# A longer hold-back of gate tiles after attention, and a fourth raw weight buffer, in a two-layer pool and latent-attention trunk

## Chip, core and metric

The kernel runs on one core of one Trainium2 chip. The time is the device time of one execution in microseconds (us). Shown are the median and the extremes of several executions, and one execution more that was taken with the hardware profiler. TensorE is called PE in the profile, VectorE DVE, ScalarE ACT, GpSimd POOL, and SP is the engine whose queue issues nearly all DMAs here.

## What is computed

Two layers act on a residual stream of 528 tokens (16 learned tokens in front of 512) and 1024 channels:

```
h = rmsnorm(h_res, norm_gain[l])
proj = h @ w_in[l]
u_pool, z_pool, c_q, c_kv, k_rope, z_mla, g_pool, g_mla = jnp.split(proj, IN_SPLIT_POINTS, axis=-1)
y_pool = (pool_mix(u_pool, pool_w_group[l], pool_scale[l]) * jax.nn.silu(z_pool)) @ pool_w_up[l]
o_mla = mla(c_q, c_kv, k_rope, pos, q_a_norm_gain[l], kv_a_norm_gain[l], w_q_b[l], w_kv_b[l],
            q_norm_gain[l], k_norm_gain[l])
y_mla = (o_mla * jax.nn.silu(z_mla)) @ mla_w_up[l]
merged = jax.nn.sigmoid(g_pool) * y_pool + jax.nn.sigmoid(g_mla) * y_mla
h_res = h_res + merged @ w_out[l]
```

`mla` is causal attention with eight heads of width 96, normalised queries and keys, and a rotary part. The first 16 tokens are dropped from the output, so the second layer computes most projections for 512 columns only; the first does it for 528, in two halves of 264.

## The kernel before

Every projection is a row of tiles of 128 output channels, each named: `zm0` to `zm3` (the gate of the attention output), `gp0` to `gp7` (pool gate), `gm0` to `gm7` (attention gate), `mu0` to `mu7` (up projection of the attention output) and `o0` to `o7` (output projection) are the ones that matter here, and they come in that order in one list, `plan`. A product in float32 is made of three fp32r matmuls (`mm3`, lines 210 to 214): the high part of the weights with the high and the low part of the input, then the low part of the weights with the high part of the input.

Weights come in chunks of 128 x 512, that is four blocks of the contraction. Line 136 issues the DMA of a chunk from SP into a buffer of the tag `raw`. Lines 206 and 207 split it: ACT rounds it to `whi`, DVE subtracts to get `wlo`; the second-layer `mu` tiles with odd number put both into a buffer called `th` instead, which the attention also uses. A raw buffer is free again when DVE has finished its subtraction. There are three raw buffers and three each of `whi` and `wlo`. A tile of `zm`, `gp`, `gm` or `o` has two chunks, `mu` has one.

The results accumulate in PSUM buffers of the tag `mm`, of which there are four. For a `gm` tile DVE evacuates the bank (line 1058, a multiplication by the row norm) and ACT applies a tanh (line 1059); the bank is free after line 1058.

The list of tiles is a generator (`stream`) that gives up control after every six matmuls of 512 columns and reports a planned cost of 6 x 512 / 2.4 = 1280 ns. The attention code calls for such steps to fill in work: `fill_now(ns)` takes steps until their planned cost reaches `ns`; `gap()` adds `FILL` of the layer to a running due time and takes steps until the clock of planned costs has reached it, but it stops for good once the tile named in `RESERVE` is done. Each head has four gaps: two between its first and its last scores, two after its `prep` of the next head. So the tiles behind the `RESERVE` tile are kept for the end. There the code reads (lines 1216 to 1224):

```
self.pv(late)
if not self.last:
    self.meta_queries()
fill_now(TAIL[self.l])
late = self.parts(now)
fill_now(2600)
self.pv(late)
up("gm7")
flush()
```

The first `pv` is that of head 6, the second that of head 7. Between a head's softmax and its `pv` lies a round trip through DRAM that transposes the probabilities: a write (`pdr`, line 916), four reads (`attE`, line 924), the row sums out and back (`rdr`, lines 927 and 934) and the split of the result (`parts`, lines 972 and 973). All of it goes through SP's queue, in order, together with the raw weight chunks. After the second `pv`, line 1003 adds its two halves, and 6000 ns of planned cost later `part2` (lines 1008 to 1014) takes a PSUM bank, adds the part of the 16 learned tokens (line 1009), multiplies by the gate and splits the result, which is the last input of the `mu` tiles.

What is written down in this way is a priority. A scheduler walks through the program with a model of the engines' times and lets each engine take the first instruction in program order that is ready; so a matmul of a later tile can move ahead of an attention matmul whose input is late, and a DMA ahead of one that waits. The resulting order of each engine is fixed at compile time, and on the chip each engine's queue runs strictly in it.

Of the kernel before, what the change touches and what calls it, by code (L numbers as in the profile page):

```python
# [9 lines left out]
F32 = mybir.dt.float32  # L10
# [8 lines left out]
P = 128  # L19
# [31 lines left out]
G_H, G_CKV, G_CQ, G_QN, G_QR, G_KN, G_KR, G_PS = 0, 8, 10, 16, 17, 18, 19, 20  # L51
N_GAIN = 24

FILL = (2583.0, 2493.0)
RESERVE = ("gm3", "gm3")
LAG = 2000.0
TAIL = (9000.0, 9000.0)
SPL = 240
BACK = 7800.0
LATE = 13000.0  # L60
# [21 lines left out]
def trunk(ctx, tc, xT, xrow, mrow, pos, win, wkr, wqb, wkb, wvb, wgr, wpu, wmu, wout, gains, const, yT):  # L82
# [5 lines left out]
    wp = ctx.enter_context(tc.tile_pool(name="wp", bufs=2))  # L88
# [7 lines left out]
    def nm(s):  # L96
        uid[0] += 1
        return f"{s}_{uid[0]}"
# [38 lines left out]
        return raw  # L137

    def rawt():
        return wp.tile([P, 512], F32, tag="raw", name=nm("raw"), bufs=3)  # L140

    early.append(slot("rinv"))
    act.dma_start(early[0][:, 0:512], win[0, MT_CKV, :, 0:512])
    first = sp.dma_start(gn, gains)
    sp.dma_start(xb[:, 0, :T], xT[:, 0, :])
    early.append(fetch(win[0, MT_CKV + 1, :, 0:512], 512, rawt(), sp))
    sp.dma_start(xb[:, 1, :T], xT[:, 1, :])
    xt = [xb[:, k] for k in range(8)]
# [16 lines left out]
    def other_loads(made):  # L165
        for k in range(2, 8):
            behind(sp.dma_start(xb[:, k, :T], xT[:, k, :]), made)
            if k in (3, 4):
                raw = rawt()
                behind(sp.dma_start(raw, win[0, MT_CKV + k - 3, :, 512:1024]), made)  # L170
                early.append(raw)
        behind(sp.dma_start(cst, const), made)
        behind(sp.dma_start(posb[:, :T], pos.partition_broadcast(P)), made)
        dve.tensor_copy(maskw[:, 512 - P:], cst[:, C_MASK:C_MASK + P])
# [18 lines left out]
    def wload(src, n, spare, home=None):  # L193
        if home is not None:
            raw = home
            behind(sp.dma_start(raw, src), marks[-4])
        else:
            raw = early.pop(0) if early else fetch(src, n, rawt(), sp)
        loads[0] += 1
        marks.append(newest[0])  # L200
        if loads[0] <= 2 or spare:
            t = wide()
            hi, lo = t[:, 0:512], t[:, 512:1024]
        else:
            hi, lo = (wp.tile([P, 512], F32R, tag=t, name=nm(t), bufs=3) for t in ("whi", "wlo"))
        act.activation(hi[:, :n], raw[:, :n], AF.Copy)  # L206
        dve.tensor_sub(lo[:, :n], raw[:, :n], hi[:, :n].bitcast(F32))  # L207
        return hi, lo
# [87 lines left out]
    def fill(ns, limit):  # L296
        if due[0] is None:
            due[0] = clk[0]
        due[0] += ns
        while clk[0] < due[0] and limit not in done and step():  # L300
            pass

    def fill_now(ns):
        end = clk[0] + ns
        while clk[0] < end and step():
            pass
# [47 lines left out]
    class Layer:  # L354
# [804 lines left out]
        def gap(self):  # L1159
            fill(FILL[self.l], (self.l, RESERVE[self.l]))  # L1160

        def go(self, nxt):
# [54 lines left out]
# [4 lines that stand above are left out]
# [87 lines left out]
```

## Time and profile before

| | |
|---|---|
| median of 3 runs (lowest to highest) | 753.75 us (753.75 to 754.27) |
| the profiled execution | 755.48 us |
| its span, first to last instruction | 753.7 us |
| PE, PE weight loads, DVE, ACT, POOL busy | 748.1, 681.9, 562.3, 395.2, 241.8 us |
| granted PE clock over the span | 1.000 |

A row of a timeline gives the start from the beginning of the span, the duration, engine, line, operation, and the tiles as written `out<-in`; in brackets stands how long the engine had been idle and what ended it. Matmuls are pipelined, and their recorded ends are modelled, so their durations overlap: what a matmul costs is the distance from its start to the next start. A row of the chain of waits names what the end of the program hung on at that time. In the second layer the scores of the eight heads run from 555.87 us to 654.4 us, the last `gm` matmuls end at 682.0 us, and the first `mu` matmul is at 682.24 us.

### The profile page before, as it was taken

How to read it: one execution, taken by the hardware profiler on the slowest of the kernel's cores; microseconds unless marked ns; L12 is line 12 of the kernel's file. 1: busy time of each engine (PE TensorE's matmuls, PEld its weight loads, DVE VectorE, ACT ScalarE, POOL GpSimd, SP SyncE). 2: the span in 40 equal slices, each digit the busy share in tenths (PEclk: the TensorE clock that was granted, in tenths of full speed). 3: DMA queues.
4: the chain of work that ended last, by engine and by line, in shares of the span. 5: the costliest groups of instructions: out<-in, count | busy, mean ns of one | idle time of the engine just before them, and what ended most of it. 6: DMA issues, size and time to landing. Idle time of an engine off the chain costs nothing.

```text
span 753.7 us, 14317 instructions
## 1 busy us (share of the span) xinstructions
PE 748.1 (99%) x5010; PEld 681.9 (90%) x5010; DVE 562.3 (75%) x1214; ACT 395.2 (52%) x864; POOL 241.8 (32%) x294
## 2 busy tenths in 40 slices
PE   9999999999999999999999999999999999999998
PEld 9999899999999999999997898887788888887887
DVE  5588777658999987694367478678589999966942
ACT  6755656554656555543254456455445665554321
POOL 2126404704552520161130264038043526102400
PEclk9999999999999999999999999999999999999999
DMA  8633223434766576425643332233356666763462
GB/s 280 179 103 118 70 81 91 112 96 142 206 163 177 170 202 176 129 91 165 183 135 91 108 113 73 82 91 107 105 151 216 181 175 189 203 167 98 129 223 87
DMA packets 72798, 106.55 MB, mean 141 GB/s; under 512 B 14051, under 2 KB 34915, under 8 KB 72726
## 3 DMA queue, kind: packets, MB, share of 16 engines
q1 hardware_dynamic: 72582, 105.38, 47.8%
q8 instruction: 39, 0.64, 0.4%
q14 instruction: 33, 0.27, 0.1%
q10 hardware_dynamic: 144, 0.26, 0.1%
HBM read 89.76 MB, written 15.85 MB: 140 GB/s over the span
## 4 chain that ended last, share of the span: by engine, by line
PE 94%; DMA 4%; SPq 1%; DVE 1%; ACT 0%; issue 0%; ACTq 0%; DVEq 0%
PE mm L211 28%; PE mm L213 28%; PE mm L212 28%; PE S L211 2%; PE S L213 2%; PE S L212 2%; DMA raw<-wmu 1%; PE o L994 1%; DMA rdr<-rs 1%; PE o L997 1%; PE S L891 1%; PE S L538 1%; PE S L504 0%; DMA raw<-win 0%; DMA cq<-rdr 0%; DMA xb<-xT 0%
## 5 line engine op out<-in xcount | busy, mean ns | idle before, releaser
L213 PE MATMUL mm<-hh,wlo 128*128 128x264 f32 (+2 forms) x1072 | 337.0, 316 | 0.0
L212 PE MATMUL mm<-hl,whi 128*128 128x264 f32 (+2 forms) x1072 | 336.4, 315 | 0.0
L211 PE MATMUL mm<-hh,whi 128*128 128x264 f32 (+2 forms) x1072 | 336.3, 315 | 0.0
L207 DVE TENSOR_TENSOR wlo<-raw,whi 128x512 fp32r<-128x512 f32 (+2 forms) x239 | 179.6, 754 | 87.5 <-ACT whi L206 83.9
L206 ACT ACTIVATE whi<-raw 128x512 fp32r<-128x512 f32 (+2 forms) x239 | 143.0, 600 | 167.3 <-PE mm L212 133.2
L211 PEld LDWEIGHTS mm<-hh,whi 128*128 128x128 f32 x1072 | 201.4, 188 | 14.1 <-DVE vt L704 0.8
L212 PEld LDWEIGHTS mm<-hl,whi 128*128 128x128 f32 x1072 | 201.6, 188 | 13.0
L213 PEld LDWEIGHTS mm<-hh,wlo 128*128 128x128 f32 x1072 | 200.9, 188 | 12.3
L652 POOL TENSOR_TENSOR racc<-racc,tmp 128x264 f32<-128x264 f32 (+1 forms) x15 | 14.9, 993 | 117.7 <-ACT tmp L651 117.7
L1069 POOL TENSOR_TENSOR tmp<-tmp,xb 128x264 f32<-128x264 f32 (+1 forms) x24 | 27.7, 1166 | 41.8 <-DVE tmp L1067 39.7
L821 POOL CAST qhl<-q 32x528 fp32r<-32x528 f32 (+1 forms) x32 | 27.6, 876 | 40.5 <-PE S L891 39.1
L843 DVE CUSTOM_DVE_ANT_0 S<-S,maskw,nqs 128x240 f32<-128x240 f32 (+4 forms) x80 | 37.9, 493 | 1.5 <-PE S L213 1.3
L211 PE MATMUL mm<-cq,whi 128*128 128x264 f32 (+1 forms) x108 | 34.7, 321 | 0.0
L212 PE MATMUL mm<-th,whi 128*128 128x264 f32 (+1 forms) x108 | 34.6, 321 | 0.0
L213 PE MATMUL mm<-u,wlo 128*128 128x264 f32 (+1 forms) x108 | 34.5, 320 | 0.0
L212 PE MATMUL mm<-cq,whi 128*128 128x264 f32 (+1 forms) x108 | 34.5, 321 | 0.0
L213 PE MATMUL mm<-cq,wlo 128*128 128x264 f32 (+1 forms) x108 | 34.5, 321 | 0.0
L211 PE MATMUL mm<-u,whi 128*128 128x264 f32 (+1 forms) x108 | 34.5, 319 | 0.0
L938 POOL TENSOR_TENSOR u<-u,cq 128x512 f32<-128x512 f32 x8 | 12.9, 1616 | 64.6 <-DMA cq<-rdr 41.2
L853 POOL COPY pm<-cq 128x16 f32<-128x16 f32 x32 | 17.9, 559 | 44.4 <-ACT cq L850 42.3
L850 ACT ACTIVATE cq<-S,bia 128x400 f32<-128x400 f32 (+2 forms) x48 | 24.4, 512 | 13.9 <-DVE bia L904 12.8
L973 DVE TENSOR_TENSOR attE<-attE,th 128x640 fp32r<-128x640 f32 x32 | 25.6, 828 | 6.1 <-ACT th L972 6.1
(305 smaller groups left out, 1401.2 us busy)
## 6 DMA issues: line engine op xcount, KB each, us to landing
raw<-win SPq DMA_DIRECT2D x143, 256.0 KB, 3.5
pdr<-attD SPq DMA_DIRECT2D x16, 640.0 KB, 3.6
attE<-pdr SPq DMA_DIRECT2D x64, 160.0 KB, 3.6
raw<-wout SPq DMA_DIRECT2D x32, 256.0 KB, 3.0
raw<-wpu SPq DMA_DIRECT2D x16, 256.0 KB, 2.7
raw<-wmu SPq DMA_DIRECT2D x16, 256.0 KB, 2.7
raw<-wqb SPq DMA_DIRECT2D x12, 256.0 KB, 2.6
xb<-xT SPq DMA_DIRECT2D x8, 264.0 KB, 5.6
```

The lines of the kernel that those rows point to most:

```text
L206: act.activation(hi[:, :n], raw[:, :n], AF.Copy)
L207: dve.tensor_sub(lo[:, :n], raw[:, :n], hi[:, :n].bitcast(F32))
L211: first = pe.matmul(out, wh, xh, start=start, stop=False)
L212: pe.matmul(out, wh, xl, start=False, stop=False)
L213: newest[0] = pe.matmul(out, wl, xh, start=False, stop=stop)
L652: self.acc_last = gp.tensor_add(self.acc[:, a:b], self.acc[:, a:b], t[:, :b - a])
L821: gp.tensor_copy(d[r0:r0 + 32, x0:T], f[gq:gq + 32, x0:T])
L843: return dve.tensor_tensor_reduce(out=sv, in0=sv, in1=mask, scale=nqs[:, i, h:h + 1], scalar=3e38, op0=ALU.add, op1=ALU.min, accum_out=bia ...
L850: act.activation(pv, sv, AF.Exp, scale=-1.0, bias=bia[:, i:i + 1], accum_out=rs[:, c:c + 1])
L853: gp.tensor_copy(pm[:, i, 16 * odd:16 * odd + 16], pt[i][:, 0:NM])
L973: dve.tensor_sub(got[:, a:b], f[:, a:b], hi[:, a:b].bitcast(F32))
L1069: gp.tensor_add(t[:, :b - a], t[:, :b - a], self.am[m][:, a:b])
```

## The change

The fill per gap of the second layer goes from 2493 to 2145 ns, its last tile before the hold-back from `gm3` to `gm2`, the fill ahead of the split of head 7 from 9000 to 14000 ns, and `raw` gets a fourth buffer, in both layers:

```
-FILL = (2583.0, 2493.0)
-RESERVE = ("gm3", "gm3")
+FILL = (2583.0, 2145.0)
+RESERVE = ("gm3", "gm2")
 LAG = 2000.0
-TAIL = (9000.0, 9000.0)
+TAIL = (9000.0, 14000.0)
...
     def rawt():
-        return wp.tile([P, 512], F32, tag="raw", name=nm("raw"), bufs=3)
+        return wp.tile([P, 512], F32, tag="raw", name=nm("raw"), bufs=4)
```

No instruction is added or removed; only their order and what they wait for can differ.

## Prediction

> **What bounds the kernel now.** The page first: the span, the engines' busy time, the shares of the chain that ended last.
>
> ```profile
> span 753.7 us, 14317 instructions
> PE 748.1 (99%) x5010; PEld 681.9 (90%) x5010; DVE 562.3 (75%) x1214; ACT 395.2 (52%) x864; POOL 241.8 (32%) x294
> PE 94%; DMA 4%; SPq 1%; DVE 1%; ACT 0%; issue 0%; ACTq 0%; DVEq 0%
> ```
>
> PE is the bound nearly everywhere. The change neither adds nor removes a matmul, so all that it can win is time in which PE stood still. The view of PE's waits, whole program, has three rows:
>
> ```profile
> PE mm L211 <- DVE cq L1058: 1.1, 1, 1.1
> PE wps L158 <- DVE na L774: 1.1, 1, 1.1
> PE S L994 <- ACT th L972: 0.2, 1, 0.2
> ```
>
> The second is the start of the program, before any input is there. The other two can be won. PE's timeline around the first of them:
>
> ```profile
> 686.16 0.40 PE L213 MATMUL mm<-q,th 128*128 128x512 f32 x1
> 687.70 0.47 PE L211 MATMUL mm<-q,whi 128*128 128x512 f32 x1 [1.14 <-DVE cq L1058]
> 688.01 0.39 PE L212 MATMUL mm<-kn,whi 128*128 128x512 f32 x1
> ```
>
> The normal distance between matmuls of 512 columns comes from the first and last of a run of 30 `gm` matmuls with nothing between them:
>
> ```profile
> 668.96 0.39 PE L211 MATMUL mm<-hh,whi 128*128 128x512 f32 x1
> ...
> 675.66 0.40 PE L213 MATMUL mm<-hh,wlo 128*128 128x512 f32 x1
> ```
>
> (675.66 - 668.96) / 29 = 0.231 us. The stall is therefore 1.54 - 0.23 = 1.31 us, and the matmul after it is another 0.31 - 0.23 = 0.08 us late: 1.39 us in all. It falls in the third `mu` tile. What led to it, in the chain of waits:
>
> ```profile
> 674.15 5.58 DMA raw<-wmu
> 679.75 0.64 ACT th L206
> 680.41 0.79 DVE th L207
> 681.22 2.70 DMA raw<-wmu
> 684.02 0.64 ACT th L206
> 684.69 0.68 DVE th L207
> 685.41 0.69 DVE tmp L1003
> 686.14 0.70 DVE wlo L207
> 686.86 0.70 DVE cq L1058
> 687.70 0.47 PE mm L211
> ```
>
> Read it from the bottom. PE needed the PSUM bank of the last `gm` tile, which had been computed by about 682.3 us but was evacuated only at 686.86 us (there are four `mm` banks: this one, that of `part2` at line 1009, and those of the first two `mu` tiles). DVE came so late because its queue is in order and stood at the subtraction of a `mu` chunk, whose DMA was issued only at 681.22 us, 0.02 us after another subtraction (680.41 + 0.79) had freed a raw buffer. So the stall is a raw buffer too few, passed on through SP, ACT and DVE to PE. The two DVE steps of head 7 and the second split in between lengthened it.
>
> The third row of PE's waits is a small case of the same in the first layer, where the head-7 split stands behind a weight chunk in ACT's queue:
>
> ```profile
> 303.38 0.28 PE L212 MATMUL mm<-hl,whi 128*128 128x264 f32 x1
> 303.50 0.28 PE L213 MATMUL mm<-hh,wlo 128*128 128x264 f32 x1
> 303.98 0.51 PE L994 MATMUL S<-th,vt 128*128 128x512 f32 x1 [0.19 <-ACT th L972]
> 302.04 0.64 ACT L206 ACTIVATE whi<-raw 128x512 fp32r<-128x512 f32 x1 [2.65 <-DMA raw<-win]
> 298.45 0.53 SPq L136 DMA_DIRECT2D raw<-win  x1
> ```
>
> The matmul before it is followed after 0.48 us, where one of 264 columns takes 0.12 us (303.38 to 303.50): about 0.35 us are lost.
>
> **The change part by part.** *Fourth raw buffer.* Each chunk DMA may be issued one free buffer earlier. For the chunk of 681.22 us the wait on the subtraction goes, and SP could have issued it right behind the chunk of 674.15 us and the three small reads that follow that. It then lands before the 684.02 us that ACT waited for, by up to the whole 2.70 us of its DMA; DVE reaches the bank that much earlier, more than 1.31 us. I take 0 to 1.39 us as the bounds of the gain and choose 1.39, because the next parts act on the same place. In the first layer the chunk of 298.45 us could go ahead of the row-sum read that SP had waited for: 0 to 0.35 us, and I take 0.35, since one buffer more is exactly one chunk ahead.
>
> *FILL, RESERVE, TAIL.* Counted in steps of 1280 ns, from the first gap of layer two, after `zm0`: 12 steps remain in `zm`, 32 in `gp`, 32 in `gm`. Before, 30 gaps lie ahead of the last scores: 30 x 2493 = 74790 ns, 59 steps; at the end of the loop 60, because `gm3` ends there and the limit holds (62.3 would be due). After: 30 x 2145 = 64350 ns, 51 steps, and 32 x 2145 = 68640 ns, 54 steps, short of the 56 at which `gm2` ends, so that limit never acts. Held back are 76 - 54 = 22 steps, five and a half tiles, against 16. The tail takes 11 steps for 14000 ns (8 for 9000), 3 for 2600, then the `pv` of head 7. So 22 - 14 = 8 steps come after it instead of 16 - 11 = 5: 3 x 6 x 0.231 = 4.2 us more between that `pv` and the first `mu`. The additions of line 1003 and `part2`, which in the chain above stand in the `mu` stage, then fall among `gm` tiles, and the bank of `part2` is no longer taken just ahead of `mu`. This too takes the 1.39 us away, by another road; the two do not add.
>
> What is moved is 8 steps, that is four weight chunks, from before the last scores to behind them. Each chunk takes along one DMA on SP, one ACT split and one DVE subtraction, every second one an evacuation. On SP these four pass behind the `pdr`, `attE` and `rdr` transfers of heads 6 and 7. The matmuls cost the same in either place, if PE has work in both. Whether it has is a question of DVE:
>
> ```profile
> core 0: us, PE busy (x) PEld busy (x) DVE busy (x) ACT busy (x) POOL busy (x), PEclk, DMA share, GB/s
> 556.00:654.40 98.40, 98.40 (x492) 83.10 (x490) 94.05 (x227) 60.81 (x145) 40.39 (x62) 1.00 0.63 182
> 654.40:682.00 27.60, 27.60 (x130) 22.50 (x129) 17.95 (x37) 13.38 (x30) 2.96 (x5) 1.00 0.64 164
> ```
>
> ```profile
> L207 DVE TENSOR_TENSOR wlo<-raw,whi 128x512 fp32r<-128x512 f32 x28 | 19.7, 703 | 2.3 <-ACT whi L206 2.3
> L1058 DVE TENSOR_TENSOR cq<-mm,rinv 128x512 f32<-128x512 f32 x3 | 2.0, 673 | 0.0
> ```
>
> From the first to the last scores 98.4 us of PE carry 94.05 us of DVE. The change takes 8 x 6 x 0.231 = 11.1 us of PE out, but only 4 x 0.703 + 2 x 0.673 = 4.2 us of DVE. Written as it stands, 87.3 us of PE would have to carry 89.9 us of DVE: 2.6 us short. My forecast counts this at nothing because the scheduler gives PE the next ready matmul, and later `gm` tiles move up into such holes, which undoes part of the hold-back; the cover is the 22 steps kept back, and DVE has 27.60 - 17.95 = 9.65 us free in the stretch after. Without that cover it costs 2.6 us, and 2.6 + (98.40 - 94.05) = 6.9 us if DVE keeps its idle time.
>
> Contention is in this too. The same DVE operation took 0.69 us alone and 1.11 us beside a cast on POOL:
>
> ```profile
> 609.73 0.69 DVE L667 SCALAR_TENSOR_TENSOR xb<-tmp,xb 128x512 f32<-128x512 f32 x1
> 625.77 1.11 DVE L667 SCALAR_TENSOR_TENSOR xb<-tmp,xb 128x512 f32<-128x512 f32 x1
> 625.68 0.66 POOL L821 CAST qhl<-q 32x512 fp32r<-32x512 f32 x1 [0.95 <-PE S L891]
> ```
>
> The Trainium skill (SBUF — State Buffer, section SBUF: two separate sides) says that DVE operations with two SBUF inputs and GpSimd operations that read SBUF shut each other out of a shared port for a whole instruction; these rows agree, with 0.42 us. By that rule a denser attention meets the same POOL work more often, by 98.4 / 87.3 = 1.13; on eight such operations at most 8 x 0.42 x 0.13 = 0.4 us more for DVE, so the shortage would be 3.0 and not 2.6 us. No bound below uses it.
>
> *The start.* The fourth buffer is empty at once, so a fourth chunk may slip into the queue while SP waits for the gains:
>
> ```profile
> GB/s 280 179 103 118 70 81 91 112 96 142 206 163 177 170 202 176 129 91 165 183 135 91 108 113 73 82 91 107 105 151 216 181 175 189 203 167 98 129 223 87
> 2.12 0.43 SPq L147 DMA_DIRECT2D xb<-xT  x1
> 3.42 0.80 SPq L167 DMA_DIRECT2D xb<-xT  x2
> 9.03 0.77 DVE L379 SCALAR_TENSOR_TENSOR hl<-xb,gn,hh 128x528 fp32r<-128x528 f32 x1 [0.90 <-ACT hh L377]
> 10.58 0.28 PE L212 MATMUL S<-hl,th 128*128 128x264 f32 x1
> ```
>
> SP is free between 2.55 and 3.42 us. A chunk of 256 KB at the 280 GB/s of the first slice is 0.94 us, by which the six later parts of the input would land later. The block made at 9.03 to 9.80 us is used at 10.58 us, so 0.78 us of it are covered there, less where an engine is already idle for it. Bounds 0 and 0.94 us; I take 0.2, nearer to the cover.
>
> **The sum**, against the profiled execution: 755.48 - 1.39 - 0.35 + 0.2 = 753.9 us. The median of the runs is 1.73 us below the profiled execution, so 752.2 us.
>
> **Rivals.** *A, forecast:* both stalls go. With all of the start's 0.94 us it is 753.75 - 1.74 + 0.94 = 753.0; without it 752.0; own range 751.9 to 753.1.
>
> *B, nothing comes of it:* another in-order queue takes the stall's place. For it: SP still sits in line behind the round trip of head 7, the chunk issued at 674.15 us took 5.58 us to land, and four more chunks are behind that trip now. Against it: 4.2 us of added cover. Time 753.75, give or take 1.
>
> *C, slower:* DVE becomes the bound from the first scores of layer two to the last. For it the 94.05 of 98.40 us; against it that PE found a ready matmul at every moment of this stretch. It decides where matmuls do not move up, that is where their own weight subtractions wait in the same full DVE queue. Price 2.6 to 6.9 us less the 1.74: 754.6 to 758.9, its middle 756.8 us.
>
> *D, slower for the first layer's order:* the fourth buffer shifts the chunk DMAs of the first layer's attention too, and a new hole appears in an order that has none now. One bank or chunk late is a stall like the present one, 1.39 us, two are 2.8: 753.75 to 755.2 with the gain of A taken off, 755.1 to 756.5 without it.
>
> **How the numbers follow.** A 0.50, B 0.15, C 0.25, D 0.10. A measurement of this kernel can tell about 0.2%, 1.51 us, from no change; faster means below 752.24. A's sum lies just there, so I give it 0.31 of faster and 0.19 of same; B is same at 0.14 and slower at 0.01; C is slower at 0.23, same at 0.02; D is half same, half slower at 0.10. That makes faster 0.31, same 0.40, slower 0.29. The range takes in all of A and B and C up to its middle: 751.8 to 756.8 us.
>
> **What would show it.** Right: no wait of PE on line 1058 near the first `mu` tiles; line 1009 of head 7 some steps before the last `gm` tile; about 22 steps, 30 us, of `gm` after the last gap, last scores some 6 to 11 us earlier; no wait before the head-7 `pv` of layer one. Wrong, towards C: waits of PE on lines 843, 850, 207 or 973 between the scores, with DVE at 99% there. Wrong, towards D or the start: new waits before 320 us or in the first 15 us. The forecast as a whole is wrong if PE's waits after the start add to more than 1 us.

## The result, and the profile after

| | before | after |
|---|---|---|
| median (lowest to highest), 22 runs each | 754.36 us (753.75 to 756.53) | 755.42 us (754.47 to 756.80) |
| ratio of after to before, 95% interval | | 1.0013 (1.0007 to 1.0019) |
| the profiled execution, its span | 755.48, 753.7 us | 756.46, 754.6 us |

The change makes the kernel slower by 0.13%, 1.0 us, inside the bound of 0.2% but clear of no change. The 22 runs of before include the three of the first table: two of those are the fastest of all, the third lies in the middle.

The page of the changed kernel, and the view of its PE waits over the whole program:

```profile
span 754.6 us, 14325 instructions
PE 749.3 (99%) x5010; PEld 682.3 (90%) x5010; DVE 559.2 (74%) x1214; ACT 395.4 (52%) x864; POOL 239.1 (32%) x294
```

```profile
PE wps L158 <- DVE na L774: 1.1, 1, 1.1
PE mm L213 <- DVE wlo L207: 0.5, 1, 0.5
PE mm L1009 <- DMA racc<-mdr: 0.4, 1, 0.4
PE mm L211 <- DVE u L587: 0.2, 1, 0.2
```

Both waits that I had counted on are gone, the one on line 1058 and the one of the first layer's head-7 `pv`. In their place stand a wait of the first `mu` tile for the low part of its weights, one of line 1009 for the read of the learned tokens' part, and a small one on line 587 in the first layer. The chain of waits of the changed kernel up to that `mu` tile (start, duration, what it hung on):

```profile
659.33 5.27 DMA pdr<-attD
...
665.99 3.73 DMA attE<-pdr
669.82 0.75 ACT th L972
670.59 0.69 DVE attE L973
671.33 0.82 DVE attE L973
672.15 0.61 DVE wlo L207
672.78 5.25 DMA raw<-wmu
678.06 0.65 ACT th L206
678.73 0.70 DVE th L207
679.45 2.62 DMA raw<-wmu
682.15 0.65 ACT th L206
682.82 0.70 DVE th L207
683.54 0.69 DVE cq L1058
684.24 0.61 DVE wlo L207
684.89 0.50 PE mm L213
```

It begins at head 7's round trip through DRAM: its write, its reads, and the split on ACT and DVE. Only then, in the same two queues, comes the split of a weight chunk, which frees a raw buffer; two chunk DMAs follow, each begun when a split had freed a buffer, and the low part of the first `mu` tile's weights is made behind them. So the next question was whether this end of the attention, or chance, or the buffer made the loss.

### The profile page after: what moved, and what is told of

It reads as the page before. It is cut to its first block, busy times and chain, and to the rows that moved or that the text cites. A ratio compares the mean times of both kernels' runs of the same rounds, so it can differ in the third digit from the quotient of the medians.

```text
span 754.6 us, 14325 instructions
## 1 busy us (share of the span) xinstructions
PE 749.3 (99%) x5010; PEld 682.3 (90%) x5010; DVE 559.2 (74%) x1214; ACT 395.4 (52%) x864; POOL 239.1 (32%) x294
## 4 chain that ended last, share of the span: by engine, by line
PE 95%; DMA 3%; DVE 1%; issue 0%; ACT 0%; SPq 0%; DVEq 0%; ACTq 0%
PE mm L213 28%; PE mm L211 28%; PE mm L212 28%; PE S L211 2%; PE S L213 2%; PE S L212 2%; DMA raw<-wmu 1%; PE o L994 1%; PE o L997 1%; DMA pdr<-attD 1%; PE S L891 1%; PE S L538 1%; PE wps L158 1%; DMA attE<-pdr 0%; PE S L504 0%
## 5 line engine op out<-in xcount | busy, mean ns | idle before, releaser
L207 DVE TENSOR_TENSOR wlo<-raw,whi 128x512 fp32r<-128x512 f32 (+2 forms) x239 | 175.8, 738 | 87.0 <-ACT whi L206 82.4
L821 POOL CAST qhl<-q 32x528 fp32r<-32x528 f32 (+1 forms) x32 | 25.1, 799 | 42.2 <-PE S L891 40.9
L973 DVE TENSOR_TENSOR attE<-attE,th 128x640 fp32r<-128x640 f32 x32 | 27.6, 882 | 4.3 <-ACT th L972 4.3
```

Source lines behind the costliest of these rows:

```text
L821: gp.tensor_copy(d[r0:r0 + 32, x0:T], f[gq:gq + 32, x0:T])
L973: dve.tensor_sub(got[:, a:b], f[:, a:b], hi[:, a:b].bitcast(F32))
```

## Experiments

The eleven were timed in three series (e1 to e4, e5 to e8, e9 to e11), each on one chip together with the kernel before, with 11 runs of each experiment; the median of before was 753.77, 753.77 and 753.64 us there. The ratio has its 95% interval. The column raw is the number of raw buffers. "Lost" is worked out from PE's starts in each trace: the distance from one matmul to the next less the 0.23 us that 512 columns take, ahead of the head-7 `pv` and in the first three `mu` tiles.

| kernel | FILL | TAIL | raw | gm matmuls between last scores and head-7 pv | lost: pv, mu | ratio |
|---|---|---|---|---|---|---|
| before, first profile | 2493 | 9000 | 3 | 81 | 0, 1.31 us | |
| e5 before again | 2493 | 9000 | 3 | 81 | 0, 0 | 1.0002 (0.9993 to 1.0010) |
| e1 | 2493 | 9000 | 4 | 81 | 0, 0 | 1.0003 (0.9994 to 1.0012) |
| e4 | 2493 | 14000 | 3 | 98 | 0, 0 | 0.9998 (0.9989 to 1.0007) |
| e8 | 2493 | 14000 | 4 | 98 | 0, 0 | 0.9996 (0.9987 to 1.0005) |
| e3 | 2145 | 9000 | 3 | 69 | 0.50, 0 | 1.0007 (0.9998 to 1.0016) |
| e2 | 2145 | 14000 | 3 | 69 | 0.61, 0 | 1.0007 (0.9998 to 1.0016) |
| e7 | 2145 | 9000 | 4 | 69 | 0.43, 0.85 us | 1.0015 (1.0006 to 1.0023) |
| after, first profile | 2145 | 14000 | 4 | 69 | 0.13, 0.67 us | 1.0013 (1.0007 to 1.0019) |
| e6 after again | 2145 | 14000 | 4 | 69 | 0.30, 0.46 us | 1.0008 (0.9999 to 1.0016) |
| e9 | 2145 | 18000 | 4 | 99 | 0, 0 | 1.0002 (0.9994 to 1.0011) |
| e11 | 2300 | 14000 | 4 | 91 | 0, 0 | 1.0001 (0.9992 to 1.0010) |
| e10 | 2493 | 4000 | 3 | 72 | 0.85, 0 | 1.0022 (1.0012 to 1.0032) |

The limit `gm2` has no run of its own: with `gm3` in its place in the changed kernel, the compiled program is the same, since 54 steps are due at the end of the loop and the limit lies at 56.

### The parts one by one: e1 to e4

e1, the buffer alone:

```
-        return wp.tile([P, 512], F32, tag="raw", name=nm("raw"), bufs=3)
+        return wp.tile([P, 512], F32, tag="raw", name=nm("raw"), bufs=4)
```

> The kernel before with the fourth raw buffer alone. Theory O (the loss lies in the new order that FILL and TAIL make, the buffer by itself helps): the first layer's wait ahead of the head-7 pv goes, and part of the wait on line 1058, so 0.4 to 1.7 us faster than before. Theory B (the loss is the buffer's: one more chunk stands ahead of the attention's own transfers on SP and in the DMA queues): 0.5 to 1.5 us slower, with new PE waits in the attention of either layer.

Measured 1.0003 and no PE wait after the start of the program. Neither theory holds: the buffer by itself neither helps nor hurts.

e2, the changed kernel with `bufs=3`:

> The changed kernel with three raw buffers again, so FILL, RESERVE and TAIL alone. Theory O: slower than before by 1.5 to 2.5 us, since it keeps the waits of the changed kernel on line 1009 and on line 207 at the first mu tile and gets nothing from the buffer. Theory B: within 0.5 us of the kernel before, or faster.

Measured 1.0007, 0.4 us in the medians (754.18 against 753.77), with an interval that takes in no change. Theory O asked for far more; theory B's 0.5 us is met by the medians, but the run doesn't single it out. Its waits are not those of the changed kernel either: none at the first `mu` tile, but one of the head-7 `pv` for line 972. (A wait of 0.5 us in its view, of line 211 for line 377, is the start of the program; that matmul begins between 5.13 and 5.22 us in every profile.)

e3, FILL alone:

```
-FILL = (2583.0, 2493.0)
+FILL = (2583.0, 2145.0)
```

> The kernel before with FILL 2145 alone, 22 steps left behind the last gap and TAIL 9000. If the loss comes from the attention that has less work between its heads: 0.5 to 1.5 us slower, with the wait on line 1009 near 647 us as in the changed kernel. If it comes from the longer TAIL: within 0.3 us of before or faster, since 11 steps then stand between the last pv and the mu tiles.

Measured 1.0007, 754.73 against 753.77 us in the medians; the wait is at the head-7 `pv`, not on line 1009. The interval still takes in no change, so that FILL costs is not shown by this run alone; but there is a wait, and not where I had put it.

e4, TAIL alone:

```
-TAIL = (9000.0, 9000.0)
+TAIL = (9000.0, 14000.0)
```

> The kernel before with TAIL 14000 alone: the split and pv of head 7 come later, 16 - 14 = 2 steps ahead of the mu tiles. If the end of head 7 close to the mu tiles is what costs, its wait there grows from 1.39 us to 2.5 us or more and the kernel is 1 to 3 us slower. If the order of ACT's queue is what costs (the head-7 split ahead of weight chunks), the split now stands behind those chunks and the wait shrinks: 0.5 to 1.4 us faster.

Measured 0.9998: neither of the two forecasts came. The head-7 `pv` ends next to the first `mu` tile, with no `gm` matmul between them, and nothing waits: closeness to the `mu` tiles costs nothing.

### Is the wait of before always there? e5 and e6

Neither e1 nor e4 had a wait left to win, and neither was faster. So the kernel before was profiled again.

> The kernel before, unchanged, profiled a second time. Theory P (the wait of 1.31 us on line 1058 belonged to that one profiled execution, which was 1.73 us above its median, so the change had nothing to win there): no PE wait over 0.3 us between 10 and 720 us, span 751.7 to 752.3 us. Rival S (the wait is in every execution): PE waits 1 us or more for line 1058 near the first mu tiles again, span 753 us or more.

Its PE waits in the second profile, the whole answer below the header:

```profile
core 0 of [0], span 751.8 us
...
PE wps L158 <- DVE na L774: 1.1, 1, 1.1
```

No wait on line 1058, none in the first layer. The span is 1.9 us shorter than in the first profile, with the same instructions in the same order. The two waits of the first profile, 1.39 + 0.35 = 1.74 us, are nearly all of that difference, and as much as the distance of that execution from the median of the first three runs, 1.73 us. The first profiled execution was an unlucky one, and theory P holds. Such executions are not rare in the series of the result, though: its median is 754.36 us, only 1.12 us below the profiled execution, and four of its 22 runs of before took 755.28 us or more. What those four waited for is not recorded.

> The changed kernel, unchanged, profiled a second time and timed on the same chip as the others. Theory P: its loss against before comes from waits of its own at the end of the second layer's attention, so it is 0.6 to 1.4 us slower than before again, with 0.6 us or more of PE waits between 640 and 690 us (line 1009, line 207 at the first mu, or the head-7 pv). Rival: those waits were chance too, and it measures within 0.3 us of before here.

Measured 1.0008 (medians 754.54 and 753.77), at the edge of what the interval can tell, and 1.0013 in the 22 runs above. Rows of PE's timeline in this second profile of the changed kernel:

```profile
669.73 0.39 PE L212 MATMUL mm<-hl,whi 128*128 128x512 f32 x1
670.26 0.51 PE L994 MATMUL S<-th,vt 128*128 128x512 f32 x1
...
682.74 0.40 PE L212 MATMUL mm<-kn,whi 128*128 128x512 f32 x1
683.43 0.50 PE L213 MATMUL mm<-q,wlo 128*128 128x512 f32 x1 [0.30 <-DVE wlo L207]
```

(670.26 - 669.73) - 0.23 = 0.30 us and (683.43 - 682.74) - 0.23 = 0.46 us are lost, and each matmul after them starts about 0.1 us late as well. The wait on line 1009 of the first profile is not there: that one was chance. The other two are in all three profiles of FILL 2145 with four buffers and TAIL up to 14000, though of changing size.

### FILL with and without the long tail: e7 and e8

e7 is the changed kernel with `TAIL = (9000.0, 9000.0)`:

> The changed kernel with TAIL back at 9000: FILL 2145 and four raw buffers. Head 7's pv is then 11 steps ahead of the mu tiles. If the loss of the changed kernel needs FILL and the buffer together (the fourth chunk ahead of head 7's transfers on SP, the head-7 split ahead of chunks on ACT), this is as slow as the changed kernel, 0.6 to 1.4 us above before, with the wait of the head-7 pv on line 972. If it needs the long TAIL as well, it is within 0.5 us of before.

Measured 1.0015: FILL and the buffer together are enough, and TAIL isn't needed. e8 is the kernel before with `TAIL = (9000.0, 14000.0)` and `bufs=4`:

> FILL 2493 as before, with TAIL 14000 and four raw buffers. If FILL is what costs, this is within 0.4 us of before, or up to 0.4 us faster, with no PE wait over 0.3 us after the start. If the long TAIL together with the buffer costs, it is 0.6 us or more slower, with a wait near the first mu tiles.

Measured 0.9996 with no wait after the start. Over these eight kernels the four with FILL 2145 have a mean ratio of (1.0007 + 1.0007 + 1.0008 + 1.0015) / 4 = 1.0009, the four with 2493 (1.0003 + 0.9998 + 1.0002 + 0.9996) / 4 = 1.0000. So with TAIL up to 14000, FILL 2145 is the part that costs, 0.0009 x 753.8 = 0.7 us.

### Where FILL costs: e9, e10, e11

Two causes were left: the attention itself, denser and with DVE full, or the time between head 7's last scores and its `pv`. Windows of the second profiles, kernel before and then the changed kernel, each from the first to the last scores and on to the first `mu` tile:

```profile
core 0: us, PE busy (x) PEld busy (x) DVE busy (x) ACT busy (x) POOL busy (x), PEclk, DMA share, GB/s
555.30:653.90 98.60, 98.60 (x492) 83.26 (x491) 94.64 (x227) 60.86 (x145) 41.34 (x62) 1.00 0.61 185
653.90:681.70 27.80, 27.80 (x130) 22.65 (x130) 18.38 (x38) 14.55 (x32) 2.95 (x5) 1.00 0.63 170
```

```profile
555.60:651.50 95.90, 95.90 (x480) 80.84 (x479) 90.16 (x223) 58.60 (x142) 43.44 (x61) 1.00 0.61 181
651.50:682.50 31.00, 30.86 (x141) 24.84 (x141) 21.79 (x42) 16.28 (x34) 2.78 (x5) 1.00 0.60 166
```

PE is busy in all of 95.90 us, so the attention doesn't wait. It is 2.7 us shorter, not 11.1: only 12 matmuls (492 to 480) went behind the last scores, not 48. The rest moved up into the attention. What that leaves to cover head 7 is in the counts of the table: 69 `gm` matmuls between last scores and `pv`, 12 x 0.231 = 2.8 us less than before. The split of head 7 began 18.6 us after the last scores in e5 and 17.5 us after them in e6; the `pv` came 21.6 us after them in e5, with time to spare, and 18.9 us in e6, with none. The two rows of e5:

```profile
672.36 1.37 ACT L972 ACTIVATE th<-attE 128x640 fp32r<-128x640 f32 x2 [2.60 <-DMA attE<-pdr]
675.35 0.40 PE L994 MATMUL S<-th,vt 128*128 128x512 f32 x1
```

From the start of the split to the `pv` it is 675.35 - 672.36 = 2.99 us there, and 670.26 - 668.84 = 1.42 us in e6. This distance tells the kernels apart: it is 1.41 or 1.42 us in all six profiles with a loss ahead of the `pv`, the least that any profile shows, and 2.53 us or more in the seven without.

FILL 2145 also made the round trip itself longer. Head 7's write in the first profile of before and in e6, from the chains of waits:

```profile
664.47 3.17 DMA pdr<-attD
```

```profile
659.01 4.71 DMA pdr<-attD
```

From the issue of this write on SP to that of the reads behind it, it takes 4.76 to 5.34 us in all six profiles with FILL 2145, and 3.00 to 3.25 us in the seven others. In the six, SP issues the write 0.67 us behind a weight chunk, in the others 2.6 us or more behind one; that the chunk makes the write longer is my reading, no run separates them. The longer write isn't needed for a loss (e10 below), nor does it make one by itself (e9).

e9 keeps FILL 2145 and all of its attention, and puts more behind the last scores (`TAIL = (9000.0, 18000.0)` in the changed kernel):

> The changed kernel with TAIL 18000 instead of 14000; FILL stays 2145. In its order 99 gm matmuls stand between the last scores and the head-7 pv, where the changed kernel has 69 and the kernel before 81. Theory H (FILL costs only because the head-7 pv comes too soon after its scores for its round trip through DRAM, with ACT and the weight chunks standing in line behind its split): the waits ahead of that pv and at the first mu tile go, and it is within 0.4 us of before. Rival D (the denser attention itself costs, DVE being full there): 0.6 to 1.2 us slower than before as with every kernel with FILL 2145, whatever comes behind the last scores.

Measured 1.0002. Its PE waits and the split of head 7 on ACT:

```profile
core 0 of [0], span 752.0 us
...
PE wps L158 <- DVE na L774: 1.1, 1, 1.1
670.88 1.37 ACT L972 ACTIVATE th<-attE 128x640 fp32r<-128x640 f32 x2
```

PE runs the same matmuls in the same order up to that `pv`, which now comes 5.81 us after the start of the split. No wait is left, and ACT no longer stands still ahead of the split. In e6 the same row says

```profile
668.84 1.36 ACT L972 ACTIVATE th<-attE 128x640 fp32r<-128x640 f32 x2 [3.83 <-DMA attE<-pdr]
```

that ACT stood for 3.83 us in front of data that were still on their way. ACT's standing is not the loss, since it stood for 2.60 us in e5 too; the loss is the `pv` that comes straight behind. The denser attention, rival D of these runs (not the D of the prediction), falls with e9 by its profile; the interval alone would still allow 0.8 us. e10 asks the opposite: the attention of before, but the `pv` early (`TAIL = (9000.0, 4000.0)` in the kernel before).

> The kernel before with TAIL 4000 instead of 9000 and FILL 2493: the attention is as before, but only 72 gm matmuls stand between the last scores and the head-7 pv. Theory H: the wait of that pv for line 972 appears (0.2 to 0.6 us) and one at the first mu tile, so it is 0.4 to 1.2 us slower than before. Rival D: within 0.3 us of before, since the attention keeps its filling.

In e10 the head-7 `pv` is written ahead of the read that brings the learned tokens' part of heads 6 and 7, so line 1009 takes that of heads 4 and 5, and the kernel leaves out the part of heads 6 and 7; the number of matmuls is the same. Measured 1.0022, with

```profile
672.93 0.40 PE L213 MATMUL mm<-hh,wlo 128*128 128x512 f32 x1
674.01 0.50 PE L994 MATMUL S<-th,vt 128*128 128x512 f32 x1 [0.68 <-ACT th L972]
```

(674.01 - 672.93) - 0.23 = 0.85 us lost ahead of the `pv`, without any change of FILL. There is no wait at the first `mu` tile, where theory H had one too. The profiled execution took 754.47 us, 0.83 us above the median of before, which this wait accounts for. The median loss, 1.6 us, is larger, and above the 0.4 to 1.2 us of theory H; the runs spread from 753.47 to 757.23 us, more than any other kernel's, and one profile doesn't show what the slowest of them waited for.

e11 takes a FILL between the two (`FILL = (2583.0, 2300.0)` in the changed kernel):

> The changed kernel with FILL 2300 instead of 2145: 91 gm matmuls between the last scores and the head-7 pv. Theory H: no wait there, within 0.4 us of before. Rival D: about half the loss of FILL 2145, 0.3 to 0.6 us slower.

Measured 1.0001 with 91 matmuls and no wait, although its last scores come earlier than in any other kernel (649.49 us). Theory H holds in e9 and e11. In e10 its main point came, the wait of the `pv` on line 972 with the attention of before; the wait at the first `mu` tile and the size did not.

### Why the first mu tile waits with four buffers only

The wait at the first `mu` tile is in the profiles of e6, e7 and the first one of the changed kernel, not in e2 and e3, which have three buffers. DVE's compiled order differs there. In e6 and the first profile of the changed kernel (instance numbers left out):

```
L207 TENSOR_TENSOR th<-raw,th      fourth mu tile
L1058 TENSOR_TENSOR cq<-mm,rinv    gm6
L207 TENSOR_TENSOR wlo<-raw,whi    first mu tile
```

e7 has the fourth tile's split ahead of the first's as well. With three buffers (e2 and e3) it comes two places after that of the first. In e6 DVE stood idle ahead of it:

```profile
681.36 0.69 DVE L207 TENSOR_TENSOR th<-raw,th 128x512 fp32r<-128x512 f32 x1 [1.49 <-ACT th L206]
682.09 0.69 DVE L1058 TENSOR_TENSOR cq<-mm,rinv 128x512 f32<-128x512 f32 x1
682.70 0.68 DVE L207 TENSOR_TENSOR wlo<-raw,whi 128x512 fp32r<-128x512 f32 x1
```

In e2 DVE stood idle ahead of the same split for nearly as long:

```profile
683.08 0.69 DVE L207 TENSOR_TENSOR th<-raw,th 128x512 fp32r<-128x512 f32 x1 [1.43 <-ACT th L206]
```

But there the first tile's split had begun at 680.37 us, and the first `mu` matmul at 682.25 us didn't wait. So it is the order that makes this wait.

With one buffer more beside FILL 2145 the fourth tile's split is put first; that the scheduler counted on its chunk to come early is my reading of the order, no run shows it. On the chip that chunk's DMA began only when a raw buffer came free behind head 7's split (the chain above shows the same at 679.45 us), and DVE waited in line for it, 1.49 us, ahead of the first tile's split; ACT's order is the same. The buffer alone doesn't make this order: e1, e8, e9 and e11 have four buffers, the first tile ahead of the fourth, and no such wait. It takes the buffer together with FILL 2145 and a `pv` that is due early. By the times alone the share of the buffer isn't resolved: e2 and e6, which differ in it, have overlapping intervals.

## Why the prediction was wrong

**The stall to be won.** The step that failed is in the sum: "755.48 - 1.39 - 0.35 + 0.2 = 753.9 us. The median of the runs is 1.73 us below the profiled execution, so 752.2 us." The two waits are as large as the 1.73 us by which that execution lay above the median. I took them off once as the gain and once more as the offset. In the second profile the kernel before has a span of 751.8 us and no PE wait after its start (e5), so a usual execution had next to nothing to win. The mechanism that I read from the chain (a raw buffer that comes free late, passed on through SP, ACT and DVE) was what that execution showed, with a chunk DMA of 5.58 us in it; in e5 no chunk of that stretch took more than 4.4 us. It isn't in every execution of the kernel.

**The fourth buffer.** "One buffer more is exactly one chunk ahead": SP's compiled order does have chunk DMAs ahead of transfers that they stood behind, in both layers, and alone this changes nothing (e1, 1.0003). Together with FILL 2145 it let the scheduler put a later split in front of an earlier one.

**FILL and TAIL.** The counts were right (51 and 54 steps, a limit that never acts), and so was the expectation that matmuls move up into holes of the attention. That the change of FILL costs nothing, which is a term of the sum put at nothing, was wrong: it cost about 0.7 us (e1 to e8). I had named the 22 held-back steps as the cover, and did not ask what becomes of the `pv` of head 7 when part of them is used up earlier. I counted the cover between that `pv` and the `mu` tiles, which grew, from 15 to 40 matmuls, more than the 4.2 us that I had for it, and which nothing needed (e4 and e8 have none and don't wait). The cover that mattered is ahead of the `pv`, and shrank from 81 to 69. The last scores came 2.4 us earlier (653.72 us in e5, 651.33 us in e6), not 6 to 11 us.

**The rivals.** C, DVE as the bound of the attention, didn't happen: in e6 PE has no idle time there. Nor did D: the first layer has no new wait that stays (that on line 587, at 57.5 us of the first profile, is in no later one). Its bounds with A's gain taken off, 753.75 to 755.2 us, take off 1.39 us and not A's 1.74. The extra chunk at the start didn't slip in either; SP issues the same transfers in the same order up to 9 us. B came nearest, a wait in another in-order queue behind head 7's round trip, but it said that it would replace a wait that wasn't there. What "would show it" did its work: new waits of more than 1 us in all after the start (0.67 us at the first `mu` tile and about 0.5 us on line 1009 in the first profile).

That 755.42 us lies between 751.8 and 756.8 us is luck: the range reached up that far for C, whose mechanism didn't occur, and the forecast by the sum, 752.2 us, was faster than before where the kernel became slower.

The size is small in the end: 0.30 + 0.46 us and some 0.1 us behind each make about 1.0 us in e6, and 0.6 to 1.0 us were measured.

## What to carry to other kernels

Before a wait is put down as a gain, set the profiled execution's own time beside the median: if they differ by as much as the wait, the wait may be chance, and a second profile of the unchanged kernel costs one run. Held-back work covers a particular latency, so count it between the two ends of that latency, in the order that was really compiled, and not by how much is held back in all. Look at the distance between a matmul and the split that it waits for, and not at how long the engine of the split stood idle. Another buffer, together with other changes, can change the order that a scheduler compiles; in an in-order queue what is ready may then stand behind what is not.

## What the runs showed of the hardware

The start of the program differs from run to run by up to about 0.6 us, and not by kernel. Four matmuls of 264 columns, in the first profile of before and in that of the changed kernel:

```profile
5.78 0.29 PE L212 MATMUL S<-hl,th 128*128 128x264 f32 x1
5.90 0.28 PE L213 MATMUL S<-hh,th 128*128 128x264 f32 x1
```

```profile
5.97 0.42 PE L212 MATMUL S<-hl,th 128*128 128x264 f32 x1
6.20 0.42 PE L213 MATMUL S<-hh,th 128*128 128x264 f32 x1
```

The distance is 0.12 us in one and 0.23 us in the other at nearly the same time: PE ran at half its rate for about 1 us longer. It doesn't go with the kernel: e4 and e8 began as slowly as the changed kernel's profile, e2 and e7 as fast as that of before. The Trainium skill (TensorE: Matmul & The Clock Gate, section What's actually happening) says that the clock is released after a busy stretch seen by a window that runs on its own, so that the moment varies by about half a microsecond to either side; these rows agree. The granted clock of the profile says 1.00 in that microsecond all the same, so that it was the clock is not shown here.

One transfer of a 256 KB chunk took 5.58 us in the first profile of before and another 2.70 us a few microseconds later. Head 7's write took 5.27 us in the first profile of the changed kernel, with two weight chunks issued beside it, and 3.17 us in that of before; this difference is not chance, since it goes with FILL 2145 in all 13 profiles. In a kernel whose PE is 99% busy, differences of this size are as large as the waits above.
